# The second layer's MLP as seven block products: sums of blocks made ahead, middle blocks kept in DRAM

## The chip, the cores and the metric

One NeuronCore of a Trainium2 chip runs the whole two-layer network in one launch. The metric is the device time of that launch in microseconds (us), the median of several runs. Engines are named as in the profile: PE is TensorE's matmul, PEld its weight load, DVE is VectorE, ACT ScalarE, POOL GpSimd, SP SyncE, which here only issues DMAs.

## What is computed

The reference is a two-layer network on 256 context and 1024 latent tokens of width 1024. The part that the change rewrites is the MLP of the second layer (`layer == 1`), which runs on the 1024 latent tokens alone, and the norm before it and the last norm after it:

```python
hl2 = _modulate(_rmsnorm(xl, norm2_g[layer]), mod_l[3], mod_l[4])
xl = xl + mod_l[5] * _sqrelu_mlp(hl2, mlp_w1[layer], mlp_w2[layer])
...
return _rmsnorm(xl, final_g)

def _sqrelu_mlp(h, w1, w2):            # h 1024x1024, w1 1024x4096, w2 4096x1024, f32
    return jnp.square(jax.nn.relu(h @ w1)) @ w2
```

## The kernel before

Features lie on the 128 partitions and tokens on the free axis. A product in f32 precision is made of three fp32r matmuls: each operand is split in a high part, rounded to fp32r, and the rest, and high x high, high x low and low x high are added up in one PSUM bank. A weight tile of 128 x 1024 is loaded by SP into a `raw` buffer (`wprep`, L138), rounded by ACT into `w[:, 0]` (L140), and the rest goes by DVE into `w[:, 1]` (L141). We call these two a prep. `WStream` keeps two tiles prepared ahead of use (`fill`, `get`). `gemm` (L165) multiplies one weight tile with eight 128 x 512 token tiles: 24 matmuls (L170 to L172).

The MLP (`mlp`, L555) goes over 16 blocks `b` of 256 hidden features. For each it loads two tiles of w1 and two of w2. Up: per hidden tile and chunk of 512 tokens one `gemm`, then Relu, Square and a copy to high on ACT (L549 to L551) and the rest on DVE (L552). Down: `gemm2` (L508), per chunk and each of eight output tiles `d` six matmuls (L518 to L520), and `acc_x` (L501, L504) adds the bank times the gate to the residual `xl` on DVE. So the hidden never leaves the chip's SBUF. In the second layer there are two chunks (`LAT_CH`); the last two blocks run chunk by chunk, the second chunk in halves of 256 tokens (`tail`), so that the last norm (`final`, L1458) overlaps.

Norms are generators that are queued (`queue`, `K.bg`) and advanced a step or more at each `tick` between matmul groups: squares on ACT, sums on DVE (L187), four matmuls with ones (L192), a power on POOL (L195), transposes that spread it (L199), then DVE and ACT per tile. The norm of the second chunk before the MLP runs beside block 0 of the first chunk. In the first layer's MLP (`layer0_in`) the same `WStream.get` also takes a step of `K.side`: conditioning tiles (`ada_tile`, L82, L85) that DVE multiplies.

The order of instructions of an engine is made at build time by a scheduler that takes, of what it thinks is ready, the earliest written; priorities (`high_priority`) move some ahead. On the chip each engine's queue then runs in that order.

Of the kernel before, what the change touches and what calls it, by code (L numbers as in the profile page):

```python
# [19 lines left out]
NC_ = 256  # L20
NL = 1024
# [8 lines left out]


class Ctx:
    pass


def setup(ctx, tc, A):
    K = Ctx()
    nc = K.nc = tc.nc
    K.tc, K.A, K.side, K.bg, K.rate, K.nacc = tc, A, iter(()), iter(()), 0, 0
    PS = bass.MemoryType.PSUM  # L40
# [90 lines left out]


def wprep(K, src):
# [41 lines left out]

def rstd_steps(K, pool, xt, c0, n, ready=lambda: KT, evac=True):
    nc = K.nc
    while not ready():
        yield
    acc = pool.tile([128, 512], F32, name="nacc", tag="nacc", bufs=2)  # L180
    nc.scalar.activation(out=acc[:, :n], in_=xt[0][:, c0:c0 + n], func=AF.Square)
    for d in range(1, KT):
        while ready() <= d:
# [414 lines left out]
def tpool(K, name, bufs=1, side=None):  # L598
    return K.tc.tile_pool(name=name, bufs=bufs, side=side, reuse_waits="tile")
# [34 lines left out]
def queue(K, rate, *gens):  # L634
    K.rate, K.bg = rate, chain(K.bg, *gens)
# [17 lines left out]
def layer0_in(K, e0, dbg):  # L653
    nc, A = K.nc, K.A
    H, L = hl_tiles(K)
    apool = e0.enter_context(tpool(K, "ada"))
    with tpool(K, "n0") as np_:
        sT = np_.tile([128, KT, 2], F32, name="sT")
# [99 lines left out]
    with tpool(K, "t4") as p4:  # L758
# [551 lines left out]
def layer1(K, dbg, out):  # L1310
# [129 lines left out]
    if dbg in ("y1", "gla"):  # L1440
        xs.close()
        return
    with tpool(K, "n6") as np_:
        gemm2(K, 1, 2, [ws.get()], [(H[7], L[7])], xt, c0, n)
        queue(K, 3, norm_steps(K, np_, 1, 1, xt, c0, n))
        c0, n = LAT_CH[1]
        for d in range(KT):
            acc_x(K, 1, 2, d, xt, gemm(K, ws.get(), H, L, c0, n), c0, n)
        drain(K)
        queue(K, 0, norm_steps(K, np_, 1, 1, xt, c0, n))  # L1450
        with tpool(K, "t6") as p4, tpool(K, "wx6") as K.wx:
            tail = (LAT_CH[:1], ((NC_ + 512, 256), (NC_ + 768, 256)))
            mlp(K, p4, 1, xt, LAT_CH, 1, tail, 2, lambda c0, n, ready: final(K, np_, xt, out, c0, n, ready))
    xs.close()


def final(K, pool, xt, out, c0, n, ready):
    nc = K.nc  # L1458
    rs = yield from rstd_steps(K, pool, xt, c0, n, ready, False)
    for d in range(KT):  # L1460
# [138 lines left out]
```

## Time and profile before

| | us |
|---|---|
| median of 3 runs | 3169.49 (3165.36 to 3172.66) |
| span of the profiled execution | 3158.7 |
| PE busy | 3042.5 (96%) |
| DVE busy | 1954.3 (62%) |
| ACT busy | 1178.8 (37%) |
| POOL busy | 261.8 (8%) |
| DMA, mean | 91 GB/s |

The span is one execution, from the first to the last instruction; the median is of timed runs, which hold what lies around the span too. A busy time is the sum over an engine's instructions. PE's instructions are pipelined: one of 512 columns lasts 0.39 us and the next starts 0.23 us after it, so counts over time say more than busy shares.

### The profile page before, as it was taken

To read this page: it belongs to the slowest core of one execution; us is meant where nothing else is said; L and a number is where in the kernel's file an instruction comes from. 1 tells how busy PE (TensorE), PEld (TensorE's weight loads), DVE (VectorE), ACT (ScalarE), POOL (GpSimd) and SP (SyncE) were. 2 spreads that over 40 slices of the span, in tenths; PEclk is the share of its full clock that TensorE was granted. 3 is DMA by queue.
4 is the path that set the end of the run, shared out by engine and by line. 5 is a ranking of instruction groups with operands and counts; after the bars stand their busy time and mean duration, and the time that the engine had idled before them with its cause. 6 is when DMAs were issued, how large, how long until landed. Compare 5 with 4: busy or idle time off the path is not lost. (4 is left out here: it accounts for less than half of the span.)

```text
span 3158.7 us, 40982 instructions
## 1 busy us (share of the span) xinstructions
PE 3042.5 (96%) x15822; PEld 2519.1 (80%) x15822; DVE 1954.3 (62%) x3583; ACT 1178.8 (37%) x2132; POOL 261.8 (8%) x384
## 2 busy tenths in 40 slices
PE   8999999999999999999988999999999999999998
PEld 4778778888888888887766777888877788888887
DVE  5896666766545455458675658786877544444446
ACT  4774233422231222235553553443444322222224
POOL 1001110000000000001065440000020000000000
PEclk9999999999999999999999999999999999999999
DMA  6333134222222222113233332332372111111113
GB/s 233 116 123 113 44 111 138 73 81 80 73 81 67 90 71 80 41 64 131 89 100 98 109 103 71 104 107 91 114 240 94 60 47 54 47 47 40 54 62 106
DMA packets 159442, 288.16 MB, mean 91 GB/s; under 512 B 35360, under 2 KB 90080, under 8 KB 159120
## 3 DMA queue, kind: packets, MB, share of 16 engines
q1 hardware_dynamic: 151248, 258.01, 25.5%
q0 software_dynamic: 7856, 27.53, 2.7%
q8 instruction: 125, 2.05, 0.3%
q14 instruction: 69, 0.57, 0.1%
q10 hardware_dynamic: 144, 0.01, 0.0%
HBM read 239.35 MB, written 41.42 MB: 89 GB/s over the span
## 5 line engine op out<-in xcount | busy, mean ns | idle before, releaser
L171 PE MATMUL mm<-hL,w 128*128 128x512 f32 (+1 forms) x2840 | 1052.9, 371 | 1.1 <-DVE hL L223 0.8
L172 PE MATMUL mm<-hH,w 128*128 128x512 f32 (+1 forms) x2840 | 1050.3, 370 | 2.6 <-DVE w L141 2.6
L170 PE MATMUL mm<-hH,w 128*128 128x512 f32 (+1 forms) x2840 | 1049.9, 370 | 2.3 <-ACT px L498 1.4
L171 PEld LDWEIGHTS mm<-hL,w 128*128 128x128 f32 x2840 | 539.5, 190 | 86.1 <-issue 3.2
L170 PEld LDWEIGHTS mm<-hH,w 128*128 128x128 f32 x2840 | 538.8, 190 | 85.7 <-ACT px L498 2.2
L172 PEld LDWEIGHTS mm<-hH,w 128*128 128x128 f32 x2840 | 539.3, 190 | 83.9 <-DVE w L141 3.5
L140 ACT ACTIVATE w<-raw 128x1024 fp32r<-128x1024 f32 x241 | 250.3, 1053 | 702.3 <-PE mm L520 617.2
L518 PE MATMUL mm<-gH,w 128*128 128x512 f32 (+1 forms) x1312 | 475.0, 365 | 5.0 <-ACT gH L551 4.9
L520 PE MATMUL mm<-gH,w 128*128 128x512 f32 (+1 forms) x1312 | 479.6, 366 | 0.0
L519 PE MATMUL mm<-gL,w 128*128 128x512 f32 (+1 forms) x1312 | 478.4, 365 | 0.1
L141 DVE TENSOR_TENSOR w<-raw,w 128x1024 fp32r<-128x1024 f32 x241 | 292.2, 1224 | 165.5 <-ACT w L140 164.8
L504 DVE SCALAR_TENSOR_TENSOR px<-mm,mod,px 128x512 f32<-128x512 f32 (+1 forms) x408 | 264.5, 660 | 203.0 <-PE mm L520 190.3
L504 DVE SCALAR_TENSOR_TENSOR xl<-mm,mod,xl 128x512 f32<-128x512 f32 (+1 forms) x296 | 211.2, 720 | 180.6 <-PE mm L520 168.8
L518 PEld LDWEIGHTS mm<-gH,w 128*128 128x128 f32 x1312 | 245.9, 188 | 48.7 <-ACT gH L551 7.2
L519 PEld LDWEIGHTS mm<-gL,w 128*128 128x128 f32 x1312 | 246.4, 188 | 43.2 <-DVE gL L552 1.0
L520 PEld LDWEIGHTS mm<-gH,w 128*128 128x128 f32 x1312 | 246.5, 188 | 40.7
L549 ACT ACTIVATE gr<-mm 128x256 f32<-128x256 f32 (+1 forms) x164 | 89.5, 546 | 468.1 <-PE mm L172 462.3
L552 DVE TENSOR_TENSOR gL<-gr,gH 128x256 fp32r<-128x256 f32 (+1 forms) x164 | 102.3, 624 | 197.2 <-ACT gH L551 197.1
L85 DVE SCALAR_TENSOR_TENSOR sdummy<-raw,sbc 128x1024 bf16<-128x1024 f32 x128 | 156.5, 1223 | 93.3 <-DMA raw<-adaT 92.1
L951 POOL TENSOR_TENSOR gtp<-gsy 80x30 f32<-80x30 f32 (+14 forms) x120 | 80.5, 671 | 232.0 <-DMA rec<-gst 113.7
L195 POOL TENSOR_TENSOR nv<-nv,mhalf 128x4 f32<-128x4 f32 (+1 forms) x14 | 15.7, 1119 | 989.5 <-DVE nv L194 989.5
L551 ACT ACTIVATE gH<-gr 128x256 fp32r<-128x256 f32 (+1 forms) x164 | 95.2, 580 | 5.0
(340 smaller groups left out, 3178.9 us busy)
## 6 DMA issues: line engine op xcount, KB each, us to landing
raw<-w SPq DMA_DIRECT2D x152, 512.0 KB
raw<-adaT SPq DMA_DIRECT2D x80, 512.0 KB
raw<-odw SPq DMA_DIRECT2D x36, 512.0 KB
raw<-wout SPq DMA_DIRECT2D x33, 512.0 KB
grec<-rec SPq DMA_DIRECT2D x32, 384.0 KB
raw<-evw SPq DMA_DIRECT2D x20, 512.0 KB
adr<-adaw SPq DMA_DIRECT2D x16, 512.0 KB
rec<-gst SPq DMA_DIRECT2D x32, 256.0 KB
```

Of the source, the lines that this page charges most:

```text
L85: nc.vector.scalar_tensor_tensor(out=dummy, in0=r, scalar=1.0, in1=s[:, w, :], op0=MUL, op1=MUL, accum_out=K.mod[l][:, ft, w:w + 1])
L140: nc.scalar.activation(out=w[:, 0], in_=raw, func=AF.Copy)
L141: nc.vector.tensor_tensor(w[:, 1], raw, w[:, 0].bitcast(F32), SUB)
L170: nc.tensor.matmul(out, w[:, 0, k, :], h, start=(k == 0), stop=False)
L171: nc.tensor.matmul(out, w[:, 0, k, :], lo, start=False, stop=False)
L172: nc.tensor.matmul(out, w[:, 1, k, :], h, start=False, stop=(k == kn - 1))
L504: K.nc.vector.scalar_tensor_tensor(out=xt[d][:, c0:c0 + n], in0=ps, scalar=K.mod[l][:, 8 * m + d, wi:wi + 1], in1=xt[d][:, c0:c0 + n], op0 ...
L518: nc.tensor.matmul(o, w[:, 0, d, :], gH, start=(f == 0), stop=False)
L519: nc.tensor.matmul(o, w[:, 0, d, :], gL, start=False, stop=False)
L520: nc.tensor.matmul(o, w[:, 1, d, :], gH, start=False, stop=(f == last))
L551: nc.scalar.activation(out=gH[:, c0:c0 + n], in_=r[:, :n], func=AF.Copy)
L552: nc.vector.tensor_tensor(gL[:, c0:c0 + n], r[:, :n], gH[:, c0:c0 + n].bitcast(F32), SUB)
```

## The change

The two matrix products of the second layer's MLP are each cut in 2 x 2 blocks and made of seven block products (Strassen's, in Winograd's form) in place of eight.

Up: hidden tiles `2q` and `2q+1` are the two columns of blocks, tokens are cut in the two chunks and features in two halves. For each of 16 `q`, each block product is `up_prod`: 12 matmuls (four feature tiles). The sums of token blocks (`ops` 4, 6, 7) are made once, by `st_norm`. The sums of weight blocks are made per `q` in the stream (`quad_srcs`): four DVE operations of 512 columns. Products 1 and 2 of the first `PRE` = 8 `q` run first (`first_quad`), while the second chunk's norm (`st_norm`) is made, and their results go to DRAM; then `up_quad` makes the rest for q < 8 (five products), and all seven for the others. The hidden's blocks and their four sums (`t1` to `t4`) are made in f32 and stored to DRAM (`K.hop`) by POOL.

Down: seven products one after the other (`order`), each over 16 steps `q` of 12 matmuls. For each step one raw tile is loaded in two DMAs, half a block of w2 (or of its sums), half the hidden block, and split as one tile by one prep. Three weight tiles are prepared ahead, with five `w` and four `raw` buffers. Banks alternate between two sets of four; a bank's partial sums are added to up to three blocks of the residual, which is read back from DRAM (`xdr`).

The sums of w2's blocks (`wsum_steps`) are made during the first layer's MLP: 32 steps, each two loads and a store by POOL and four DVE operations of 256 columns, one step at a `get`.

```diff
+    K.sdr = [[K.dram.tile([128, 4, 512], F32, ...) for q in range(NQ)] for w in range(2)]
+    K.hop = {p: [K.dram.tile([128, 512], F32, ...) for q in range(NQ)] for p in range(1, 8)}
...
 def wprep(K, src):
-    raw = K.wr.tile([128, KT, 128], F32, name="raw", tag="raw")
-    nc.sync.dma_start(out=raw, in_=src)
+        for lo, hi, ap in parts:
+            nc.sync.dma_start(out=raw[:, lo:hi], in_=ap)
+def quad_srcs(K, l, q, first):
...
+    def sums():
+        a = st[0] if first else load(0)
+        b = load(1)
+        s = rawt(K)
+        tt(s[:, 4:8], a[:, 0:4], b[:, 0:4], SUB)
+        tt(b[:, 0:4], b[:, 0:4], b[:, 4:8], ADD)
+        tt(s[:, 0:4], b[:, 0:4], a[:, 0:4], SUB)
+        tt(a[:, 4:8], a[:, 4:8], s[:, 0:4], SUB)
+        return s
+    return ([lambda: load(0)] if first else []) + [sums, lambda: st[1], lambda: st[0][:, 4:8]]
...
 class WStream: def get(self):
+                if self.K.last is not None:
+                    with self.K.tc.issue_after(self.K.last):
+                        next(self.K.side2, None)
...
 layer1:
+        with tpool(K, "n6") as np_, tpool(K, "pre") as pp:
...
+            ws = WStream(K, [A["w1"][1, 2 * q] for q in range(PRE)])
+            queue(K, 2, st_norm(K, np_, 1, xt, 1, ops))
+            for q in range(PRE):
+                first_quad(K, pp, ws.get(), q, ops)
+            drain(K)
+        K.wx = xs.enter_context(tpool(K, "wx7", side="right"))
+        rx = xs.enter_context(tpool(K, "rx7", 2, side="right"))
+        ws = WStream(K, [s for q in range(NQ) for s in quad_srcs(K, 1, q, q >= PRE)], K.wx, raws=(rx, rx))
+            for q in range(NQ):
+                up_quad(K, hp, ws, q, ops)
+        down(K, 1, xt, wx8, rx, lambda ...: final(...))
-            tail = (LAT_CH[:1], ((NC_ + 512, 256), (NC_ + 768, 256)))
-            mlp(K, p4, 1, xt, LAT_CH, 1, tail, 2, lambda ...: final(...))
+def st_norm(K, pool, l, xt, ci, ops):
+    for d in range(KT):
+        nc.gpsimd.dma_start(out=K.xdr[:, d, ...], in_=xt[d][:, c0:c0 + n])
+    rs = yield from rstd_steps(K, pool, xt, c0, n, nb=1)
...
+    for j in range(4):                 # ci == 1
+        scale(j)
+        nc.vector.tensor_tensor(x11, x12, x11, SUB)
+        scale(j + 4)
+        split(K, x22, ops[3][j], sB(j + 4))
+        stt(x12, x22, df[:, j:j + 1], x12)
+        stt(x22, x22, sB(j + 4), x11)
+        split(K, x22, ops[6][j])
+        stt(x21, x21, sB(j + 4), x22)
+        split(K, x12, ops[7][j])
+        split(K, x11, ops[5][j])
+        split(K, x21, ops[4][j])
+def up_quad(K, pool, ws, q, ops):      # here q < PRE
+        nc.sync.dma_start(out=p1, in_=K.p1dr[q])
+        nc.sync.dma_start(out=h11, in_=K.hop[1][q])
+        w = ws.get(); b2 = mm_tile(K)
+        up_prod(K, b2, w, 0, ops[6], True, False)
+        tt(u2, b2, p1, ADD)
+        w3 = ws.get(); b3 = mm_tile(K)
+        up_prod(K, b3, w3, 0, ops[5], True, False)
+        up_prod(K, b2, w, 1, ops[7], False, False)
+        tt(u3, b2, p1, ADD)
+        tt(h22, b3, u3, ADD)
+        up_prod(K, b4, ws.get(), 0, ops[3], True, True)
+        tt(u2, b3, u2, ADD)
+        tt(h12, b4, u2, ADD)
+        up_prod(K, b2, w3, 1, ops[4], False, True)
+        tt(h21, b2, p1, ADD)
...
+    for h in (h22, h21, h12):
+        sq_relu(K, h, h)
+    tt(t1, h12, h11, SUB); tt(t3, h22, h12, SUB); tt(t2, h22, t1, SUB); tt(t4, h21, t2, SUB)
+    for p, t in ((2, h21), (3, h22), (5, t1), (7, t3), (6, t2), (4, t4)):
+        nc.gpsimd.dma_start(out=K.hop[p][q], in_=t)
+def down(K, l, xt, wx, rx, after):
+    order = (1, 6, 2, 7, 5, 4, 3)
+    src = [[(0, 4, wop(p, q)), (4, 8, K.hop[p][q]...)] for p in order for q in range(NQ)]
+    ws = WStream(K, src, K.wx, wx, wx, ahead=3, raws=(rx, rx))
+    for c0, n in LAT_CH:
+        for d in range(KT):
+            nc.sync.dma_start(out=xt[d][:, c0:c0 + n], in_=K.xdr[:, d, ...])
+    for p in order:
...
+        for q in range(NQ):
+            w = ws.get()
+            rh, rl = (w[:, i, 4:8].rearrange("p k c -> p (k c)") for i in range(2))
+            for d in range(4):         # three matmuls each, into bank[key][d]
...
+        if p == 1:
+            for d0, c0 in ((0, a1), (4, a1), (4, a0)):
+                acc("A", d0, c0)
...
+        else:                          # p == 3, the last
+            drain(K)
+            K.nacc = 4
+            queue(K, 3, urgent(K, after(a1, n, lambda: K.nacc, (4, 5, 6, 7, 0, 1, 2, 3))))
+            acc("A", 0, a1)
+            drain(K)
```

The last norm of the second chunk now runs in one piece of 512 tokens, four of its eight tiles ahead of the last product's end.

## Rows read from the trace of the kernel before

**Rows 1.** The page's first part: busy time, share of the span and count of instructions of each engine.

```profile
PE 3042.5 (96%) x15822; PEld 2519.1 (80%) x15822; DVE 1954.3 (62%) x3583; ACT 1178.8 (37%) x2132; POOL 261.8 (8%) x384
```

**Rows 2.** The view by windows: window, its length, then busy us and (count) of PE, PEld, DVE, ACT, POOL, the granted PE clock, the DMA engines' busy share and GB/s. The second layer's MLP as a whole, 600 us of its middle, and 40 us near its start.

```profile
2426.00:3145.00 719.00, 712.80 (x3293) 588.06 (x3291) 345.51 (x462) 207.90 (x312) 2.94 (x2) 1.00 0.18 57
2500.00:3100.00 600.00, 599.89 (x2622) 489.60 (x2621) 270.44 (x340) 157.06 (x226) 0.00 (x0) 1.00 0.16 51
2440.00:2480.00 40.00, 34.95 (x150) 27.21 (x151) 30.68 (x42) 15.16 (x21) 1.28 (x1) 1.00 0.20 66
```

**Rows 3.** The view of waits, of PE from 2380 us to the end: engine, tile, line, whom it waited for, us in all, times, longest.

```profile
PE sm L199 <- POOL nv L195: 5.3, 4, 2.2
PE mm L518 <- ACT gH L551: 2.7, 1, 2.7
PE mm L171 <- DVE hL L223: 0.8, 1, 0.8
```

**Rows 4.** The timeline: start us, duration, engine, line, operation, out<-in, shape, then the idle time before and what ended it. Two matmuls that follow each other just before the MLP, ACT's first Relu of the MLP, and two matmuls late in it.

```profile
2424.05 0.39 PE L171 MATMUL mm<-hL,w 128*128 128x512 f32 x1
2424.27 0.39 PE L172 MATMUL mm<-hH,w 128*128 128x512 f32 x1
...
2431.50 0.60 ACT L549 ACTIVATE gr<-mm 128x512 f32<-128x512 f32 x1 [2.86 <-PE mm L172]
...
3083.86 0.40 PE L170 MATMUL mm<-hH,w 128*128 128x512 f32 x1
3084.09 0.39 PE L171 MATMUL mm<-hL,w 128*128 128x512 f32 x1
```

**Rows 5.** The view of groups by line and shape, from 2432 us to the end: count, busy us, mean ns of one, then the engine's idle time before them and what ended it.

```profile
L141 DVE TENSOR_TENSOR w<-raw,w 128x1024 fp32r<-128x1024 f32 x73 | 87.7, 1220 | 81.5 <-ACT w L140 81.5
L140 ACT ACTIVATE w<-raw 128x1024 fp32r<-128x1024 f32 x73 | 75.1, 1052 | 276.9 <-PE mm L520 276.8
L550 ACT ACTIVATE gr<-gr 128x512 f32<-128x512 f32 x60 | 37.6, 626 | 0.8
```

**Rows 6.** The timeline of DVE in three places where it runs without a gap: from one start to the next is what an instruction takes up of the engine.

```profile
2408.75 0.74 DVE L220 SCALAR_TENSOR_TENSOR nt<-xl,modA,nrs 128x512 f32<-128x512 f32 x1
2409.42 0.69 DVE L187 TENSOR_TENSOR nacc<-nacc,nsq 128x512 f32<-128x512 f32 x1
2410.02 0.74 DVE L504 SCALAR_TENSOR_TENSOR xl<-mm,mod,xl 128x512 f32<-128x512 f32 x1
...
3122.17 1.22 DVE L141 TENSOR_TENSOR w<-raw,w 128x1024 fp32r<-128x1024 f32 x1
3123.30 2.06 DVE L1462 SCALAR_TENSOR_TENSOR xl<-xl,gn,sm 128x512 f32<-128x512 f32 x3
...
3142.28 0.41 DVE L187 TENSOR_TENSOR nacc<-nacc,nsq 128x256 f32<-128x256 f32 x1
3142.61 0.48 DVE L504 SCALAR_TENSOR_TENSOR xl<-mm,mod,xl 128x256 f32<-128x256 f32 x1
```

**Rows 7.** The view by windows again, in the mixer before the MLP, where PE waits for a chain on DVE and ACT (columns as in Rows 2).

```profile
2254.00:2256.00 2.00, 1.04 (x6) 0.66 (x6) 1.69 (x6) 0.37 (x1) 0.00 (x0) 1.00 0.41 142
2256.00:2258.00 2.00, 0.68 (x5) 0.49 (x4) 1.86 (x12) 0.00 (x0) 0.00 (x0) 0.64 0.11 26
2258.00:2260.00 2.00, 1.48 (x5) 1.15 (x6) 1.82 (x3) 0.37 (x1) 0.00 (x0) 0.50 0.42 171
2260.00:2262.00 2.00, 2.00 (x8) 1.65 (x7) 1.36 (x2) 0.00 (x0) 0.00 (x0) 0.50 0.61 193
2262.00:2264.00 2.00, 2.00 (x8) 1.65 (x8) 1.56 (x5) 0.33 (x2) 0.00 (x0) 0.65 0.34 113
2264.00:2266.00 2.00, 2.00 (x11) 1.62 (x10) 2.00 (x4) 1.29 (x7) 0.21 (x1) 1.00 0.45 162
```

**Rows 8.** The view by windows in the stretch of the span in which DMA is busiest.

```profile
2305.00:2335.00 30.00, 26.04 (x147) 20.12 (x145) 20.64 (x47) 13.51 (x29) 9.07 (x17) 1.00 1.01 358
```

**Rows 9.** The view of the residual's tile `xl`: its 16 loads of 256 KB that POOL issues one upon the other in the stretch of Rows 8 (ns of POOL that an issue takes, shortest, median, longest), and the time from issue to landing.

```profile
L1428 POOL DMA_DIRECT2D xl<-xdr x16: 537/537/542, 2310.8 to 2323.4; - x16
...
DMA to landing us min/median/max: 5.4/7.6/9.0
```

**Rows 10.** The view of `raw` in the MLP: SP's issues of w1 and w2 (ns of one, shortest, median, longest).

```profile
L138 SPq DMA_DIRECT2D raw<-w x55: 327/328/328, 2503.2 to 3077.5; - x55
```

**Rows 11.** The timeline of the end, all engines but PEld: the last matmul of the MLP, its last sum, the spreading of the last norm's factor, and the last products with it.

```profile
3144.39 0.28 PE L520 MATMUL mm<-gH,w 128*128 128x256 f32 x1
...
3144.79 0.48 DVE L504 SCALAR_TENSOR_TENSOR xl<-mm,mod,xl 128x256 f32<-128x256 f32 x1
...
3148.76 0.69 PE L199 MATMUL sm<-cm,nv 128*128 128x128 f32 x2 [1.10 <-POOL nv L195]
3149.49 5.18 DVE L1462 SCALAR_TENSOR_TENSOR xl<-xl,gn,sm 128x256 f32<-128x256 f32 x13 [0.78 <-PE sm L199]
```

**Rows 12.** The view by windows in the first layer's MLP (columns as in Rows 2).

```profile
640.00:1100.00 460.00, 460.00 (x2409) 395.84 (x2408) 252.48 (x381) 117.29 (x191) 0.00 (x0) 1.00 0.24 78
```

**Rows 13.** The view of the tensor `adaT`: who waits for the loads of the side work, for how many us in all, and how often.

```profile
  DVE sdummy L85: 92.1, 58
```

More of the change, by code (lines that the diff above doesn't have):

```diff
@@ L61, in setup @@
     K.xdr = K.dram.tile([128, KT, NL], F32, name="xdr")
+    K.sdr = [[K.dram.tile([128, 4, 512], F32, name=f"sdr{w}{q}") for q in range(NQ)] for w in range(2)]
+    K.hop = {p: [K.dram.tile([128, 512], F32, name=f"hop{p}{q}") for q in range(NQ)] for p in range(1, 8)}
+    K.p1dr = [K.dram.tile([128, 512], F32, name=f"p1dr{q}") for q in range(PRE)]
     return K
@@ L130, in ada_cols, with rawt @@
             in1=K.gn[:, 0, f0 - 8:f0 - 4].unsqueeze(2).to_broadcast([128, 4, 2]), op0=ADD, op1=MUL)
+def rawt(K):
+    t = K.rl[K.ri % len(K.rl)].tile([128, KT, 128], F32, name="raw", tag="raw")
+    K.ri += 1
+    return t
 def wprep(K, src):
@@ L173, in gemm, with rstd_steps @@
     return out
-def rstd_steps(K, pool, xt, c0, n, ready=lambda: KT, evac=True):
+def rstd_steps(K, pool, xt, c0, n, ready=lambda: KT, evac=True, order=tuple(range(KT)), nb=2):
     nc = K.nc
@@ L179, in rstd_steps @@
         yield
[L180 to L183, printed above, removed]
+    acc = pool.tile([128, 512], F32, name="nacc", tag="nacc", bufs=nb)
+    nc.scalar.activation(out=acc[:, :n], in_=xt[order[0]][:, c0:c0 + n], func=AF.Square)
+    for i in range(1, KT):
+        d = order[i]
+        while ready() <= i:
             yield
@@ L201, in rstd_steps @@
         return pb
-    rs = pool.tile([128, 512], F32, name="nrs", tag="nrs", bufs=2)
+    rs = pool.tile([128, 512], F32, name="nrs", tag="nrs", bufs=nb)
     nc.scalar.activation(out=rs[:, :n], in_=pb[:, :n], func=AF.Copy)
@@ L768, in layer0_in @@
         mlp(K, p4, 0, xt, OUT_CH, 2, (OUT_CH[:2], OUT_CH[2:]), 1, after)
+        for _ in chain(K.side, K.side2):
+            pass
     return xt
@@ new lines, in layer1, with wsum_steps, load @@
+    with tpool(K, "xm") as xp_, tpool(K, "wx8", 2) as wx8, tpool(K, "n8") as np_:
+        xt = [Shifted(xp_.tile([128, NL], F32, name=f"xm{d}"), NC_) for d in range(KT)]
+        down(K, 1, xt, wx8, rx, lambda c0, n, ready, order: final(K, np_, xt, out, c0, n, ready, order))
+    xs.close()
+def wsum_steps(K, l):
+    nc = K.nc
+    todo = [(1, q, hf) for q in range(NQ) for hf in range(2)]
+    def load(i, q, hf):
+        raw = K.sr.tile([128, KT, 128], F32, name="sraw", tag="sraw")
+        for f in range(2):
+            src = K.A[("w1", "w2")[i]][l, 2 * q + f].rearrange("p (s k) c -> p s k c", s=2)[:, :, 2 * hf:2 * hf + 2]
+            nc.gpsimd.dma_start(out=raw[:, 4 * f:4 * f + 4].rearrange("p (s k) c -> p s k c", s=2), in_=src)
+        return raw
+    raw = load(*todo[0])
+    yield
+    for n, (i, q, hf) in enumerate(todo):
+        b = [raw[:, 2 * j:2 * j + 2] for j in range(4)]
+        a11, a12, a21, a22 = b if i == 0 else (b[0], b[2], b[1], b[3])
+        tt = nc.vector.tensor_tensor
+        tt(a22, a21, a22, ADD)
+        tt(a21, a11, a21, SUB)
+        tt(a11, a22, a11, SUB)
+        tt(a12, a12, a11, SUB)
+        nc.gpsimd.dma_start(out=K.sdr[i][q][:, :, 256 * hf:256 * hf + 256],
+                            in_=raw.rearrange("p (j k) c -> p j (k c)", j=4))
+        if n + 1 < len(todo):
+            raw = load(*todo[n + 1])
+        yield
@@ new lines, in up_prod, with mm_tile @@
+def up_prod(K, ps, w, half, op, first, last):
+    nc = K.nc
+    for k in range(4):
+        h, lo = op[k]
+        i = 4 * half + k
+        nc.tensor.matmul(ps, w[:, 0, i, :], h, start=(first and k == 0), stop=False, skip_group_check=True)
+        nc.tensor.matmul(ps, w[:, 0, i, :], lo, start=False, stop=False, skip_group_check=True)
+        nc.tensor.matmul(ps, w[:, 1, i, :], h, start=False, stop=(last and k == 3), skip_group_check=True)
+    tick(K)
+def mm_tile(K):
+    return K.pmm.tile([128, 512], F32, name="mm", tag="mm")
@@ new lines, in sq_relu, with first_pair @@
+def sq_relu(K, dst, src):
+    nc = K.nc
+    nc.scalar.activation(out=dst, in_=src, func=AF.Relu)
+    nc.scalar.activation(out=dst, in_=dst, func=AF.Square)
+def first_pair(K, pool, w, q, ops, between=lambda p1: None):
+    nc = K.nc
+    b1 = mm_tile(K)
+    up_prod(K, b1, w, 0, ops[1], True, False)
+    p1 = pool.tile([128, 512], F32, name="sp1", tag="sp1", bufs=2)
+    nc.scalar.activation(out=p1, in_=b1, func=AF.Copy)
+    between(p1)
+    up_prod(K, b1, w, 1, ops[2], False, True)
+    h11 = pool.tile([128, 512], F32, name="sh11", tag="sh11", bufs=2)
+    sq_relu(K, h11, b1)
+    nc.gpsimd.dma_start(out=K.hop[1][q], in_=h11)
+    return p1, h11
@@ L1461, in final @@
+def final(K, pool, xt, out, c0, n, ready, order=tuple(range(KT))):
+    nc = K.nc
+    rs = yield from rstd_steps(K, pool, xt, c0, n, ready, False, order)
+    for d in order:
         t = xt[d][:, c0:c0 + n]
```

170 lines of the change are left out of this document (150 added, 20 removed).

## The prediction

> **What bounds the kernel now.** Read the page's busy shares first [rows 1]: PE at 96% is the engine to look at, DVE at 62% the next. Then the windows of the second layer's MLP [rows 2]: PE is busy 712.8 of 719 us at full clock, DVE under half, DMA at 57 GB/s. In the middle 2622 matmuls start in 600 us, one every 0.229 us (the timeline shows steps of 0.22 and 0.23 [rows 4]). The MLP has 3072 matmuls of 512 columns, or as many columns in halves at the end: 2 products x 32 hidden tiles x 8 x 2 chunks x 3. At 0.229 us that is 703.5 us. The first hidden tile's 24 matmuls end where ACT's first Relu starts, at 2431.5, so they began at 2426.0 [rows 4]; the last ends at 3144.7 [rows 11]. So of 718.7 us some 15 are lost, most near the start, where 40 us hold 150 matmuls in place of 175 [rows 2]; the waits name few of them [rows 3]. PE alone sets this stretch, so fewer matmuls are time, if the rest can be fed.
>
> **What is removed.** Seven products in place of eight leave 7/8 of the matmuls: 2 x 16 x 7 x 12 = 2688. At 0.229 us: 615.6 us. This is 103 us under today's stretch, of which 88 are matmuls and 15 today's losses. Everything below is what the new stretch loses. For the step I allow 1%, 6 us, either way.
>
> **What an instruction of DVE costs.** From start to start a TENSOR_TENSOR of 512 columns takes 0.60 us, a SCALAR_TENSOR_TENSOR 0.67, the prep's 1024 columns 1.13, and 256 columns 0.33 [rows 6]. Reads of PSUM in TENSOR_TENSOR do not occur in these rows; I take 0.67, as for L504, which reads a bank. ACT takes 1.05 us for a prep and 0.63 for 512 columns [rows 5].
>
> **From the first 8 q to the rest.** While products 1 and 2 of eight `q` run (192 matmuls, 44 us), the second chunk's norm must be made, with its sums of blocks. The factor `rs` comes out after five `tick`s, since the matmuls with ones are written behind the fourth product: 5 x 2.75 us and an ACT copy, 14.4 us. Then DVE has per `j` six operations of 0.67 and five of 0.60, 7.0 us, four times: 28. Between them stand four preps, 4.5. That ends at 47, 3 us behind PE. Then the four sums of the first `quad_srcs`, 2.4, and ACT's prep, 1.05, with hops 51: PE stands for 7 us, since its next product needs that tile. In the mixer a gap of about 2.5 us within 4 us is followed by windows granted 0.64, 0.50, 0.50 and 0.65, so at the lower level of 1.2 GHz for a part of 8 us [rows 7]; the time lost by that is (0.36 + 0.50 + 0.50 + 0.35) x 2 = 3.4 us. I take 7 + 3.4 = 10.5; bounds 4 (some sums slip in earlier) and 18 (ACT, 0.9 loaded there by my count, holds up the splits).
>
> **The up product, q < 8.** Per quad PE has 60 matmuls, 13.7 us. DVE has the four sums and `t1` to `t4`, 8 x 0.60, six evacuations, 6 x 0.67, preps of 1.13, 1.13 and 0.6: 11.7 us, 85%. Within the quad each accumulation on a bank waits for a DVE read of it, and one product (2.75 us) lies between as cover. The prep of `b` for the next quad needs the buffer that product 4, the quad's last, frees: 1.05 + 1.22 us of ACT and DVE against 2.75 until product 5. If an evacuation comes behind that prep on DVE, the cover is overrun: 1.05 + 1.22 + 3 x 0.67 = 4.3 against 2.75, 1.5 us. The scheduler avoids some of it. The nearest rows with DVE this loaded are the 40 us near the MLP's start: DVE 77%, 25 matmuls missing, 5.7 us or 14% [rows 2], though part of it is a norm's chain. 14% of 110 us is 15. Bounds 0 and 20; I take 1 us a quad, 8. For q >= 8 PE has 84 matmuls, 19.2 us, DVE 12.2 (one prep more, one evacuation less), 63%, and two products of cover in most places: 3 us for eight quads, bounds 0 and 10. POOL's six or seven issues a quad at 0.54 us [rows 9] are under 4 us of 13.7; bytes are 3 MB in 13.7 us, 219 GB/s, under the 358 that the span shows [rows 8].
>
> **From up to down.** The first down tiles need `w` buffers freed by products 4 and 3 of the last quad, one of them a product ahead: covered but for small change. SP also loads the residual, 16 x 256 KB, 4.2 MB, some of it only when product 4 has freed the space. At 358 GB/s [rows 8] all of it takes 11.7 us, and stands in the queue ahead of the next weight tiles, but three tiles (8 us) are prepared and half of the residual's space is free early. I take 2, bounds 0 and 12.
>
> **The down product.** 112 steps of 2.75 us. ACT 1.05, DVE 1.13 and 36 sums of 0.67 spread over 308 us: half loaded. SP issues two DMAs at 0.33 [rows 10]. Bytes: 0.52 MB a step, 191 GB/s, against 57 today [rows 2] and 358 at most. Four `raw` buffers turn round in landing plus prep: with the 7.6 us at which 256 KB landed under full load [rows 9], (7.6 + 1.05 + 1.22 + 0.3) / 4 = 2.5 us, under the step; with the longest, 9.0, it is 2.9 and costs 112 x 0.15 = 17. At 191 GB/s they should land sooner. I take 2, bounds 0 and 17. The seven changes of banks are covered by a product of 44 us on the other set.
>
> **The end.** From the last matmul's end to the span's end are 14.0 us today [rows 11]. With 512 columns the last sum, square and add take 0.75 us more, two more columns of L192 and L199 0.6, eight products of 0.66 as long as today's 13 of 256 columns, the last store 0.3 more: +1.8.
>
> **The first layer.** 32 steps of 4 x 0.33 us, 43 us of DVE, in a stretch of some 455 us where DVE is idle for 45% and PE never [rows 12]. DMA goes from 78 to about 150 GB/s. Per block two `get`s follow each other at once, so a step's operations can stand on DVE waiting for a load issued just before; behind them are the sums of L504, for which PE's banks wait. DVE already waits 58 times, 92 us in all, for such loads [rows 13], and PE shows no loss. So little: I take 4; bounds 0 and 40 (eight times 5 us, the shortest landing of rows 9). Issues on POOL block no power there: no norm runs in these steps.
>
> **The sum.** 615.6 + 10.5 + 8 + 3 + 2 + 2 = 641 for 718.7: -77.6. With +1.8 and +4: -71.8. The profiled span of 3158.7 becomes 3087; the median lies 10.8 above the span, so 3169.5 - 71.8 = 3098.
>
> **Rivals.**
> (a) Almost nothing is exposed: DVE and DMA keep up, only half of the gap after the first 8 q stays. Then 5 + 19 us less is lost, 3074. For it: DVE is below 100% in every stretch but one. Against: 3 us of PE's cover per wait.
> (b) The up product is set by DVE's order. Each of 16 quads loses 2 us and after it the clock, 3.4 us more [rows 7]: 16 x 5.4 = 86 in place of 11, 3173, no change; where both waits of a quad fall behind a prep it is slower. It would decide from 5.2 us a quad. Against it: for q >= 8 DVE has a third of its time free, and PE's gaps would be shorter than in rows 7.
> (c) The first layer's sums hold up PE at each pair of `get`s and the down product's loads land at 9 us: 36 + 15 more, 3149. Half of it is likelier than all: 3125.
> (d) Slower: the down product is set by its loads. If the two DMAs of a tile land one behind the other, each at the 7.6 us of rows 9, the turn of four buffers is (15.2 + 2.6) / 4 = 4.4 us a step, 1.7 over PE, 112 x 1.7 = 190 in place of 2: 3286. It decides from a landing of 11.1 us for both: (11.1 + 2.6) / 4 is 0.66 over the step, and 112 x 0.66 eats the gain and the 2 us above. Against it: in rows 8 many transfers of this size are in flight at once and 358 GB/s come out. The Trainium skill (DMA: Bandwidth & Descriptors, "Anatomy of one DMA" and "Bandwidth") speaks for it: a DMA costs some 2.0 us besides its bytes and loads should be of 1 MiB or more, and this change halves today's 512 KB. By its formula, an estimate, 256 KB take 2.6 us, two in a row 5.2 against a step of 2.75, and the down product alone would lose 275 us; rows 8 contradict that loads wait for each other.
>
> **Chances.** The forecast and what is near it, 3080 to 3115: 0.58. (a): 0.13. (c) and the space up to 3163: 0.18. (b): 0.06, half no change, half slower. (d): 0.05. A measurement of this kernel tells about 0.2%, 6.3 us, from no change. So faster 0.89, same 0.03, slower 0.08. The range leaves out (d), (b), the end of (c) and what lies under (a), 0.19 together: 3068 to 3145.
>
> **What would show it.** Right: 2688 matmuls of 512 columns in the MLP; PE gaps of 7 to 10 us once, after the 16th product, with a window at a lower granted clock behind it, ended by DVE's sums and ACT's prep; gaps near 1 us per quad, ended by DVE; the down product at 2.75 us a step with ACT's prep waiting for PE, not for DMA; the first layer's windows as full as today. Wrong: if in the down product ACT's prep waits for loads step after step, (d); if quads are 16 us and more, (b); if PE in 640 to 1100 us shows gaps, (c); if matmuls start further apart than 0.229 us without a wait, for 190 to 220 GB/s into the same memory, a price of which I have no row beyond 358 GB/s in a stretch where PE stood still anyway.

## The result, and the profile after

The changed kernel takes 3089.27 us (median of 4 runs, 3085.7 to 3092.11), the kernel before, run beside it, 3167.43 (4 runs, 3165.36 to 3172.66): a ratio of 0.9747, with a 95% interval of 0.9733 to 0.9761. Forecast was 3098, so the change brings 78 us where 72 were expected. The profiled span goes from 3158.7 to 3083.9 us, by 74.8; each is one execution, and the one profiled before the change was a short one (see the sum, below).

The page's first part, as [rows 1]; PE still sets the time:

```profile
PE 2959.9 (96%) x15246; PEld 2444.0 (79%) x15246; DVE 2062.2 (67%) x3736; ACT 1256.8 (41%) x2176; POOL 403.5 (13%) x615
```

The windows (columns as in [rows 2]): the first layer's MLP, which answers to [rows 12]; the last 38 us of the norm beside the first products; what follows it; the up quads of q < 8; all up quads; the seam between up and down; the rest of the down product.

```profile
640.00:1100.00 460.00, 460.00 (x2401) 395.40 (x2400) 295.62 (x509) 114.09 (x185) 65.97 (x92) 1.00 0.45 149
2448.00:2486.00 38.00, 32.74 (x132) 23.85 (x132) 36.68 (x53) 27.11 (x45) 6.59 (x13) 0.99 0.53 173
2480.00:2490.00 10.00, 6.35 (x21) 4.32 (x20) 7.47 (x10) 4.38 (x6) 0.54 (x1) 0.83 0.48 159
2500.00:2600.00 100.00, 100.00 (x440) 82.33 (x439) 87.60 (x125) 49.64 (x69) 23.66 (x44) 1.00 0.65 223
2487.00:2761.00 274.00, 274.00 (x1196) 224.77 (x1195) 198.73 (x271) 126.67 (x177) 56.09 (x104) 1.00 0.55 191
2760.00:2770.00 10.00, 3.67 (x12) 2.24 (x11) 1.86 (x2) 2.78 (x3) 0.00 (x0) 0.76 0.84 325
2772.00:3067.00 295.00, 295.00 (x1301) 242.91 (x1299) 162.76 (x159) 118.26 (x118) 1.04 (x1) 1.00 0.59 191
```

In the two long stretches a matmul starts every 0.229 us, as before [rows 2], though DMA moves 191 GB/s there instead of 51 to 57: 274 / 1196 in the first, and 295 / 1289 in the second, where 12 of the 1301 are short ones of the last norm (L237, L244). Ahead of the last matmul PE loses time in two places alone, around the end of the first products (2448 to 2490) and at the seam (2760 to 2770). The waits of PE from 2400 us on name them (columns as in [rows 3]):

```profile
PE mm L1747 <- ACT w L159: 6.3, 1, 6.3
PE sm L237 <- DVE nacc L232: 3.6, 1, 3.6
PE mm L1618 <- ACT w L159: 3.4, 1, 3.4
```

L1618 is the first matmul of an up product, L1747 of a down product, L159 the prep on ACT. The 3.4 us stand is the one behind the first 8 `q`. The 6.3 us stand is at the seam, and the timeline shows who is late there:

```profile
2746.00 11.41 SPq L1727 DMA_DIRECT2D xm<-xdr  x16
2758.43 0.33 SPq L156 DMA_DIRECT2D raw<-w  x1
...
2766.90 1.06 ACT L159 ACTIVATE w<-raw 128x1024 fp32r<-128x1024 f32 x1 [13.13 <-DMA raw<-hop]
2768.01 1.22 PE L1747 MATMUL mm<-w 128*128 128x512 f32 x2 [6.29 <-ACT w L159]
...
3066.64 0.39 PE L1749 MATMUL mm<-w 128*128 128x512 f32 x1
...
3070.65 1.87 PE L237 MATMUL sm<-cm,nacc 128*128 128x1 f32 x8 [3.61 <-DVE nacc L232]
3073.86 1.12 PE L244 MATMUL sm<-cm,nv 128*128 128x128 f32 x4 [1.34 <-POOL nv L240]
```

SP issues the residual's 16 loads (L1727) one after the other, 11.4 us; behind them stands the next weight tile's load (L156), whose prep starts 8.5 us after it was issued, so four steps into the down product PE has nothing prepared. ACT, the engine that PE is said to wait for, was idle for 13.1 us itself; what is late is the load, first in SP's queue and then behind the residual's 4.2 MB. The last three rows are the end of the kernel, to be held against [rows 11].

Stage by stage, profile against profile (before, after):

| stretch | before | after | difference |
|---|---|---|---|
| start of the kernel to the first load of `evw`, a weight of the first stage | 35.7 | 39.3 | +3.6 |
| from there to the first down matmul of the first layer's MLP | 561.4 | 561.3 | -0.1 |
| to its last | 874.8 | 874.6 | -0.2 |
| to the second layer's first up matmul | 954.1 | 956.9 | +2.8 |
| the second layer's MLP | 718.7 | 634.9 | -83.8 |
| its last matmul's end to the span's end | 14.0 | 16.9 | +2.9 |

### The profile page after: what moved, and what is told of

Its sections match the earlier page's. It is cut to its first block, busy times and chain, and to the rows that moved or that the text cites. A ratio compares the mean times of both kernels' runs of the same rounds, so it can differ in the third digit from the quotient of the medians.

```text
span 3083.9 us, 41065 instructions
## 1 busy us (share of the span) xinstructions
PE 2959.9 (96%) x15246; PEld 2444.0 (79%) x15246; DVE 2062.2 (67%) x3736; ACT 1256.8 (41%) x2176; POOL 403.5 (13%) x615
## 5 line engine op out<-in xcount | busy, mean ns | idle before, releaser
L216 PE MATMUL mm<-hH,w 128*128 128x512 f32 (+1 forms) x2296 | 845.2, 368 | 3.3 <-DVE w L160 3.3
L215 PE MATMUL mm<-hL,w 128*128 128x512 f32 (+1 forms) x2296 | 847.6, 369 | 0.0
L214 PE MATMUL mm<-hH,w 128*128 128x512 f32 (+1 forms) x2296 | 844.8, 369 | 2.1 <-ACT px L543 1.4
L159 ACT ACTIVATE w<-raw 128x1024 fp32r<-128x1024 f32 (+1 forms) x341 | 351.6, 1037 | 714.2 <-PE mm L565 340.4
L160 DVE TENSOR_TENSOR w<-raw,w 128x1024 fp32r<-128x1024 f32 (+1 forms) x341 | 407.4, 1202 | 245.0 <-ACT w L159 243.0
L216 PEld LDWEIGHTS mm<-hH,w 128*128 128x128 f32 x2296 | 437.6, 191 | 65.2 <-DVE w L160 4.2
L214 PEld LDWEIGHTS mm<-hH,w 128*128 128x128 f32 x2296 | 436.8, 190 | 64.8 <-ACT px L543 2.2
L565 PE MATMUL mm<-gH,w 128*128 128x512 f32 (+1 forms) x768 | 273.2, 356 | 0.0
L564 PE MATMUL mm<-gL,w 128*128 128x512 f32 (+1 forms) x768 | 272.4, 355 | 0.1
L563 PE MATMUL mm<-gH,w 128*128 128x512 f32 (+1 forms) x768 | 269.2, 353 | 2.3 <-ACT gH L596 2.3
L563 PEld LDWEIGHTS mm<-gH,w 128*128 128x128 f32 x768 | 144.0, 188 | 24.7 <-ACT gH L596 3.1
L564 PEld LDWEIGHTS mm<-gL,w 128*128 128x128 f32 x768 | 144.0, 188 | 22.7 <-DVE gL L597 0.6
L565 PEld LDWEIGHTS mm<-gH,w 128*128 128x128 f32 x768 | 144.4, 188 | 19.3
L1747 PE MATMUL mm<-w 128*128 128x512 f32 x256 | 100.6, 394 | 6.3 <-ACT w L159 6.3
L1618 PE MATMUL mm<-hH,w 128*128 128x512 f32 x256 | 100.6, 394 | 0.9 <-ACT sp L1639 0.7
L1620 PE MATMUL mm<-hH,w 128*128 128x512 f32 x256 | 100.2, 393 | 1.1 <-DVE w L160 1.1
```

Of the source, the lines that this page charges most:

```text
L159: nc.scalar.activation(out=w[:, 0, :n], in_=raw, func=AF.Copy)
L160: nc.vector.tensor_tensor(w[:, 1, :n], raw, w[:, 0, :n].bitcast(F32), SUB)
L214: nc.tensor.matmul(out, w[:, 0, k, :], h, start=(k == 0), stop=False)
L215: nc.tensor.matmul(out, w[:, 0, k, :], lo, start=False, stop=False)
L216: nc.tensor.matmul(out, w[:, 1, k, :], h, start=False, stop=(k == kn - 1))
L563: nc.tensor.matmul(o, w[:, 0, d, :], gH, start=(f == 0), stop=False)
```

## The experiments

All start from the changed kernel. "Up" is from the first up matmul to the first down matmul, "down" from there to the start of the last: 318.5 and 316.0 us in the changed kernel, 634.5 together. Each run but the last is a single one. They are compared by these two stretches, since single whole times also carry what differs from run to run ahead of the MLP: with the residual spread out, with twelve first `q` and with late sums the whole takes 3088.29, 3085.92 and 3090.19 us, and shows none of the three gains by itself. In runs whose edit leaves it alone up takes 318.5 to 319.8 us and down 312.2 to 316.5, as the stand at the seam lasts 3.1 to 6.7 us.

**The residual's loads spread out.** Is the seam SP's queue, or the space that the loads need?

```diff
-    for c0, n in LAT_CH: for d in range(KT): nc.sync.dma_start(out=xt[d][...], in_=K.xdr[...])
...
+            if p == 1 and 1 <= q <= 8:         # behind the newest weight load
+                for d, c0 in todo[2 * q - 2:2 * q]: nc.sync.dma_start(...)
```

> The 16 loads of the residual are issued two at a time behind the weight loads of steps 1 to 8 of the first down product, in place of all ahead of the down product's fourth weight tile. Theory: PE's stand between the up and the down product (6.3 us, and some 8.4 us with the slow clock behind it) comes from SP's queue, where the 16 issues and their 4.2 MB stand ahead of the next weight tiles. Then the stand goes, under 1 us is left, and from the up product's end to the last matmul 7 to 9 us less pass. Rival 1: the stand is the turnover of ACT and DVE at the end of the last quad: it stays above 5 us. Rival 2: the loads collide wherever they stand, since the first down product needs 191 GB/s already: the stand is shared out over the first eight steps, which take 2.9 us or more each in place of 2.72.

Down takes 307.4 us, 8.6 less; up 319.5. The stand is gone, though the same bytes are moved beside the down product's first steps:

```profile
2762.30:2784.00 21.70, 21.70 (x96) 17.75 (x96) 12.72 (x13) 9.04 (x11) 2.70 (x5) 1.00 0.98 350
```

PE is full while DMA moves 350 GB/s. So not the bytes but their place ahead of the weight tiles made the seam. Spreading takes away both the late issue and the landing behind the residual, 8.5 us; which of them costs more was not tried apart. And 1344 matmuls at 0.229 are 307.8: behind the seam the down product loses nothing.

**Twelve first `q`, and four.** The first products cover the second chunk's norm. The number of `q` that they are made of, `PRE`, was set to 12, then to 4.

> Products 1 and 2 of 12 q run first, in place of 8, so PE has 66 us in place of 44 to cover the second chunk's norm. Theory: DVE's count of the norm sets the end of that stretch (about 49 us behind the MLP's start, and 2.4 + 1.05 us more). Then PE's stand of 3.4 us and the slow clock behind it go; from the MLP's start to the last matmul 4 to 8 us less. Rival: each quad of five products costs PE gaps, and four more of them (12 in place of 8, DVE 85% loaded) give the gain back: the time stays within 2 us or rises, with gaps ended by DVE in the quads 8 to 11.

> The first stretch of up products (the q before the modulated norm is ready) is cut from 8 to 4, so TensorE has some 22 us of work there and not 44. Theory: the norm of the second layer's MLP is counted out by VectorE and ends some 49 us after the first up product whatever the length of this stretch, so TensorE's stand behind it grows from 3.4 us to about 26, and from the first up product to the last down product it takes 15 to 20 us more than 634.5. Rival: the stand comes from the weight stream starting again behind the stretch; then it stays at 3 to 4 us and the total within 2 us of 634.5.

With 12 the stand of 3.4 us goes, but up takes 316.7, only 1.8 less and still 8.9 over its matmuls: what PE loses during the norm stays, and the first quads behind it now lose time (20 us from 2507.3 hold 77 matmuls, 10 fewer than at 0.229). Up and down together fall by 5.2 to 629.3, in the range expected, but by luck: 3.4 of that is the seam, which was shorter in this run and which the edit does not touch. With 4 the waits and windows are:

```profile
PE mm L1618 <- ACT w L159: 23.4, 1, 23.4
```

```profile
2460.00:2470.00 10.00, 0.60 (x3) 0.18 (x1) 9.81 (x16) 5.81 (x10) 0.54 (x1) 0.70 0.36 113
2470.00:2480.00 10.00, 0.00 (x0) 0.00 (x0) 9.93 (x16) 4.68 (x8) 0.00 (x0) 0.50 0.18 70
2480.00:2490.00 10.00, 5.92 (x17) 4.32 (x18) 7.08 (x10) 2.64 (x4) 0.00 (x0) 0.60 0.32 101
```

PE stands for 23.4 us while DVE is full, and its next product starts 48.2 us after the first; with 8 it was 53.0. So it is DVE's count of operations that ends this stretch, and the restart of the weight stream is refuted as its cause. Up and down together take 648.2, 13.7 more, under the 15 to 20 expected: the norm ends 4.8 us earlier, which the four preps fewer between its operations on DVE (4 x 1.13) would make, and the seam's stand was 3.2 here.

**The first layer's sums held back.** In the changed kernel the scheduler put the first loads of `wsum_steps` at the start of the kernel. The timeline of POOL in the changed kernel:

```profile
1.28 3.06 POOL L1527 DMA_DIRECT2D sraw<-w  x4 [0.84 <-POOLq L1838]
```

```diff
-                    with self.K.tc.issue_after(self.K.last):
+                    with self.K.tc.issue_after(self.K.last), self.K.tc.issue_after(self.K.lastx):
...
-            nc.gpsimd.dma_start(out=xt[d][:, :T], in_=A["xT"][:, d, :])
+            K.lastx = nc.gpsimd.dma_start(out=xt[d][:, :T], in_=A["xT"][:, d, :]).ins
```

> All loads for the sums of w2 are held back on POOL's queue until the first layer's residual has been loaded; nothing else changes. Theory: the 3.6 us by which the first weight tile of the first layer is loaded later than before (39.3 in place of 35.7 us) come from the first 1 MB of these loads, which now run at 1.3 us, where DMA is full: they go, and the first load of evw starts at 36 us again. Rival: the start just varies from run to run: it lies anywhere between 35 and 40 us, though no sraw load is near. In both, the first layer's MLP takes as long as before (some 887 us from the first to the last use of its hidden).

The tile's rows now begin at 476.1 us in place of 1.3:

```profile
L1527 POOL DMA_DIRECT2D sraw<-w x64: 704/716/737, 476.1 to 1080.9; - x64
```

SP's first load of `evw` is issued at 36.6 us. In the nine runs with the early loads it is at 37.8 to 41.1, before the change at 35.7, and in the last experiment below, which holds them back too, at 36.3. So the four early loads, 1 MB, cost some 3 us at the start. That it reaches the end can't be read from this run: its stretch from there to the first layer's MLP took 568.3 us in place of 561.3. This stretch differs from run to run, 561.3 to 569.3 in the nine with the early loads and 554.9 in the last experiment. The first layer's MLP itself takes 876.1 with the late loads and 874.6 with the early ones, 874.8 before: no price of the sums there.

**Two `raw` buffers in the down product.** How far is rival (d)?

```diff
-    ws = WStream(K, src, K.wx, wx, wx, ahead=3, raws=(rx, rx))
+    ws = WStream(K, src, K.wx, wx, wx, ahead=3)
```

> The down product's stream has two raw buffers in place of four. Theory (each buffer turns round in landing plus prep, 2.6 us): a step takes (L + 2.6) / 2 where that is above PE's 2.72. With a landing of the pair of 256 KB loads of 3.5 us that is 3.05 us a step, 37 us more in all; from L = 2.9 us it begins to cost. Rival (loads wait in queues, L of 7.6 us as 256 KB took in the busiest stretch of the kernel before): 5.1 us a step, 265 us more. If there is no cost, L is under 2.9 us and four buffers were never needed.

Down takes 370.9, 54.9 more; 37 were expected. The waits of ACT from 2800 to 3100 us show the expected cause, and the timeline of SP and ACT a pair of loads from its issue at 2902.08 to its prep at 2906.08 (the prep between is of the other buffer):

```profile
ACT w L159 <- DMA raw<-hop: 184.6, 87, 7.8
```

```profile
2902.08 0.33 SPq L156 DMA_DIRECT2D raw<-w  x1
2902.46 0.42 SPq L156 DMA_DIRECT2D raw<-hop  x1
2902.95 1.06 ACT L159 ACTIVATE w<-raw 128x1024 fp32r<-128x1024 f32 x1 [2.16 <-DMA raw<-hop]
...
2906.08 1.06 ACT L159 ACTIVATE w<-raw 128x1024 fp32r<-128x1024 f32 x1 [2.07 <-DMA raw<-hop]
```

A step takes (370.9 - 8.6) / 112 = 3.23 us on average; two buffers turn round in 6.47, of which 2.6 are preps and hops, so a tile's two DMAs land in 3.9 us together, not in 15.2 as rival (d) has it. The expectation had taken 3.5 for it. If they land as soon with four buffers, these turn in (3.9 + 2.6) / 4 = 1.6 us a step, under the 2.75 of PE; there the preps wait for PE and not for loads, so this landing can't be read from them.

**Every load of the down product twice.** The second load goes to buffers that nothing reads.

```diff
             w = ws.get()
+            dm = K.rd.tile([128, KT, 128], F32, ...)
+            for lo, hi, ap in src[...]: nc.sync.dma_start(out=dm[:, lo:hi], in_=ap)
```

> In each step of the down product the two loads are made a second time into a spare ring of four buffers that nothing reads: 1.05 MB a step in place of 0.52. Theory: loads overlap, so the step is bound by bytes: at the 358 GB/s of the busiest stretch before 2.93 us, 0.2 us over PE's 2.72, 20 to 25 us in all, with the DMA share at 1.0; at 390 GB/s, the most seen in 5 us, nothing. Rival (loads wait for each other): a pair of loads that takes 5 us or more, and a step of 5 us: 250 us more.

Down takes 336.2, 20.2 more, as expected. Here the DMA engines are full:

```profile
2900.00:3000.00 100.00, 96.67 (x423) 79.03 (x423) 48.12 (x46) 38.39 (x39) 0.00 (x0) 1.00 1.00 360
2960.00:2980.00 20.00, 20.00 (x89) 16.51 (x88) 8.39 (x7) 6.75 (x7) 0.00 (x0) 1.00 1.00 354
```

At 360 GB/s the 1.05 MB of a step take 2.91 us, 0.16 over PE's step, 18 in 112. But the loss does not come step by step, as the second row shows. Behind the seam it comes where products end. The waits of PE from 2800 to 3070 us come first here, then DVE's twelve sums of the first product, which stand ahead of the longest wait's prep:

```profile
PE sm L1751 <- DVE w L160: 10.3, 3, 7.0
PE mm L1751 <- DVE w L160: 3.9, 3, 1.7
```

```profile
2810.06 7.99 DVE L549 SCALAR_TENSOR_TENSOR xm<-mm,mod,xm 128x512 f32<-128x512 f32 x12 [3.31 <-PE mm L1752]
```

The changed kernel has the same 8.0 us of sums, from 2801.2 on, and no wait of PE from 2800 to 3066 us, so there the tiles prepared ahead cover them; with DMA full they no longer did. The changed kernel's 191 GB/s are about half of what this stretch bears.

**Four more sums per quad on DVE.** The sums `t1` to `t4` are made twice.

```diff
     tt(t4, h21, t2, SUB)
+    tt(t1, h12, h11, SUB); tt(t3, h22, h12, SUB); tt(t2, h22, t1, SUB); tt(t4, h21, t2, SUB)
```

> DVE makes the hidden's four sums t1 to t4 twice in each quad of the up product, the same values: 2.4 us more per quad. Theory: the up product is PE's as long as DVE's sum per quad stays under PE's, since the order of its queue leaves cover for each wait. For q < 8 DVE then has 14.1 us against PE's 13.7, so these quads grow to DVE's: 0.4 us each, 3 us in all, with DVE at 100%; for q >= 8 (14.6 against 19.2) nothing. Rival (each accumulation waits behind whatever stands on DVE): four more operations at each quad's end push the evacuations of the next quad back, 1.5 us or more in each of 16 quads, 24 us or more.

Up takes 321.7, 3.2 more where 3 were expected, for 64 operations that take 38 us of DVE. DVE is nearly full, and PE begins to lose:

```profile
2500.00:2600.00 100.00, 99.46 (x432) 80.15 (x431) 95.56 (x144) 42.62 (x63) 21.37 (x40) 1.00 0.61 205
```

So the quads of q < 8, at 87.6% of DVE, still had 12.4% of 13.7, 1.7 us of DVE each, to spare, and the order on DVE does not hold PE: rival (b) is refuted for this kernel.

**Two buffers for the up weights in place of three.** What kept the quads free of gaps?

```diff
-        ws = WStream(K, [...quad_srcs...], K.wx, raws=(rx, rx))
+        ws = WStream(K, [...quad_srcs...], raws=(rx, rx))
```

> The up products' prepared weights get two buffers instead of three; nothing else changes. Theory: a weight's preparation (rounding and a sum, about 2.0 us on ScalarE or VectorE) lies behind a product only because the third buffer is free before it; with two, the quads of q below 8, where most weights are prepared sums, show two uncovered preparations of some 2 us each, 32 us more from the first up product to the first down product (318.5), and the quads from 8 on nothing. Rival 1: the order of the instructions hides them all the same; under 8 us more. Rival 2: the quads from 8 on lose as much; up to 64 us more.

Up takes 344.7, 26.2 more; 32 were expected. The waits of PE from 2430 to 2780 us:

```profile
PE mm L1618 <- ACT w L159: 10.2, 13, 3.4
PE mm L1618 <- DVE raw L180: 7.3, 3, 2.5
```

The loss is where it was expected: the 100 us from 2500 hold 347 matmuls, those from 2640 are full (437). The waits name 17.5 us, 3.4 of them the stand that the changed kernel has too, so 14.1 of the 26.2. Slow matmuls make up at least a part of the rest, in windows and then in the timeline of PE:

```profile
2510.00:2520.00 10.00, 9.28 (x41) 7.38 (x40) 4.84 (x8) 1.96 (x4) 2.16 (x4) 1.00 0.65 234
2520.00:2530.00 10.00, 7.32 (x25) 5.23 (x24) 8.60 (x12) 4.35 (x6) 2.70 (x5) 0.83 0.61 193
```

```profile
2523.84 0.50 PE L1618 MATMUL mm<-to,w 128*128 128x512 f32 x1 [2.46 <-DVE raw L180]
...
2527.01 0.63 PE L1618 MATMUL mm<-to,w 128*128 128x512 f32 x1
2527.44 0.63 PE L1619 MATMUL mm<-to,w 128*128 128x512 f32 x1
```

Behind a gap of 2.5 us matmuls start 0.43 us apart for some 3 us, in a window granted 0.83, so a short wait here costs more than its length.

**The last down product twice.** One product's price in place, with all its loads and preps and no sums between the two:

```diff
-    order = (1, 6, 2, 7, 5, 4, 3)
+    order = (1, 6, 2, 7, 5, 4, 3, 3)     # banks start at the first, are read after the second
```

The output's last block thus holds that product twice.

> The last product of the down product is run a second time into the same banks, with its loads and preps, as an eighth product, so the block of the output that it goes to holds it twice. Theory: a product is worth PE's time for 192 matmuls: 16 x 2.72 = 43.6 us more, so the two products that the change takes away are worth 87 us and the losses at the seams take the rest. Rival (the steps are fed by DMA and preps, and PE just fits): an added product costs clearly more than 44 us, or the steps show waits on ACT.

Down takes 359.9, 43.9 more; 192 matmuls at 0.229 are 44.0. So this product costs its matmuls and nothing beside.

**The three repairs together.** Late residual, twelve first `q`, late sums.

> The late residual loads, the 12 first q and the late sums of w2 together. Theory: the three losses stand at different places and add up: 8.5 at the seam to the down product, 2 to 5 at the end of the first products, 3.3 at the start: 14 to 17 us under the changed kernel, some 3073 us, ratio to the kernel before 0.970. Rival: the start varies by itself, so only 10 to 12 us are left: 0.9715.

3075.15 us (median of 5, 3063.43 to 3080.53) against 3169.73 for the kernel before (8 runs): 0.9707, 0.9690 to 0.9725, outside the changed kernel's interval and 14 us less. Up and down together take 624.4, 10.1 less, and `evw` starts 3.0 us earlier: 13.1 of the 14. Down alone is 307.4 again. The profiled execution is the fastest of the five, though, 22.2 us shorter in its span than the changed kernel's: 6.4 of that lie between `evw` and the first layer's MLP and 2.3 between the two MLPs, where no edit is.

## Why the prediction was right, and by which steps

**Matmuls.** 615.6 forecast; at the measured pitches 1344 x 0.2291 + 1344 x 0.2289 = 615.5. The fear of a longer pitch at 190 to 220 GB/s fell: the changed kernel, and the run at 350 GB/s with PE full, show none. This term carries the gain, and the doubled product shows that it is worth what it was costed at.

**After the first 8 `q`.** 10.5 forecast. In the first 49.6 us 44.0 would have done: 5.6 lost while DVE is full (the window from 2448), of which the waits name 1.8; then the stand of 3.4; then slow matmuls, 23 missing in the 10 us from 2481.7, 5.3 with the stand. Together 10.9, and up is 10.7 over its matmuls. The size was right, and the cause of the stand (a chain on DVE that outlasts PE's work) is shown by the run with four. But in the forecast's own terms the chain ended 53.0 us after the first product's start and not 51, and the clock cost 1.9 and not 3.4; the two errors cancel. And it lay elsewhere in part: nothing was forecast inside the norm, where half of it was.

**Up quads.** 8 + 3 forecast, 0 measured (440 matmuls in 100 us, at 87.6% of DVE). This step was mis-sized: it was taken from the 40 us near the MLP's start [rows 2], whose loss, as in the changed kernel's own 38 us, came with a norm's chain. What keeps the quads free of it is the third weight buffer, which the stream of the kernel before has too (`wx6`, L1451): with two buffers the quads of q < 8 lose 26.2 / 8 = 3.3 us each, where rival (b) had 5.4.

**From up to down.** 2 forecast, 8.6 measured, inside the bound of 12: 6.3 of it the stand, the rest slow matmuls behind it (granted clock 0.76). The bound was the right mechanism, loads that stand ahead of the next weight tile, and the value taken was mis-sized: I let three prepared tiles cover them. PE ran through four steps while SP still issued and the loads landed.

**The down product.** 2 forecast, -0.4 measured behind the seam (307.4 for 307.8). As forecast the prep waits for PE there, not for loads. The waits of ACT from 2775 to 3066 us in the changed kernel:

```profile
ACT w L159 <- PE mm L1749: 82.6, 51, 2.6
ACT w L159 <- PE sm L1749: 69.5, 42, 1.7
ACT w L159 <- DMA raw<-hop: 8.3, 6, 5.6
```

The 7.6 us of [rows 9], from which its bound and rival (d) came, are of sixteen loads queued at once; the pair here lands in 3.9, and in 8.5 behind the residual's sixteen. The rule of the Trainium skill that the prediction set against the change (DMA: Bandwidth & Descriptors, "Bandwidth", loads of 1 MiB or more) did not decide: loads of 256 KB came at 191 GB/s without a wait of PE, and at 350 to 360 when asked for. The formula that the prediction took from the Trainium skill (DMA: Bandwidth & Descriptors, "Anatomy of one DMA") stands there for DMAs that POOL issues, while SP issues these; by measure a pair lands in 3.9 us and not in 5.2.

**The end.** +1.8 forecast, +2.9 measured. From the last matmul's end to the spreading of the factor it is 6.8 us now (L244), 4.1 before [rows 11]: 2.7 of the 2.9. I had counted three terms there, 0.75, 0.6 and 0.66; which one is larger was not measured apart.

**The first layer.** +4 forecast, in the MLP. There it cost nothing, as [rows 12] had let hope: 460.00 of 460 us at 149 GB/s. It cost some 3 us at a place that I had not looked at, the kernel's start, since the scheduler takes what is ready and the first loads of the sums were ready at once. I had looked at POOL's queue in the steps of the MLP only, and did not follow it back to the first instruction.

**The sum.** Forecast 641 for the MLP, measured 634.9; -74.8 between the spans for -71.8. The terms' errors are -11 for the up quads, +6.6 for the seam and -2.4 for the down product. They cancel in part, so that the total came out this close is partly luck. The 2.8 us between the two MLPs stay open: that stretch took 954.4 to 959.4 us in the ten runs above, 954.6 with all three repairs, so it is not tied to an edit. Nor was the 10.8 us between median and span a constant, as I used it: it is 5.4 after the change. What lies around a span is less: each run on record is 1.7 to 2.0 us longer than its own span. The rest is that the profiled executions were short ones, by some 9 us before the change and 3.6 after it, so the medians, with -78, are the better measure of the change. Executions of kernels that start alike differ by up to 8 us ahead of the first layer's MLP (561.3 to 569.3, above).

**Rivals.** (a) was near for the quads and the down product, but not for the seam and the norm. (b) and (d) were refuted by experiment, (c) by the profile.

## What to carry to other kernels

Count matmuls first, then list every place where a stream of prepared tiles starts, ends or is refilled: in this kernel the long stretches lost nothing, and the loss was in two seams. Look in a queue for the block of loads that isn't needed yet but stands ahead of the one that is, and spread it out; 8.6 us came back here from a few lines. When new work has no input of its own to wait for, look where the scheduler puts its first instruction.

## What the runs showed of the hardware that was not expected

Operations of one form differ in pace. Among DVE's sums of weight blocks (L177 to L180) one starts 0.72 us after the other, while the hidden's (L1704, L1705) take up 0.60, both 128 x 512 in f32 with all operands in SBUF and with the same 0.69 us of duration. The timeline of DVE in the changed kernel:

```profile
2561.21 0.69 DVE L178 TENSOR_TENSOR raw<-raw 128x512 f32<-128x512 f32 x1
2561.94 0.69 DVE L179 TENSOR_TENSOR raw<-raw 128x512 f32<-128x512 f32 x1
2562.66 0.69 DVE L180 TENSOR_TENSOR raw<-raw 128x512 f32<-128x512 f32 x1
...
2571.77 0.69 DVE L1704 TENSOR_TENSOR st<-sh,sh 128x512 f32<-128x512 f32 x1
2572.37 0.69 DVE L1705 TENSOR_TENSOR st<-sh,st 128x512 f32<-128x512 f32 x1
2572.97 0.69 DVE L1666 TENSOR_TENSOR su<-mm,sp 128x512 f32<-128x512 f32 x1
```

L179 reads what L178 has just written, and L180 what L179 has; L1705 and L1666 don't read what the operation before them wrote. The same trace has the same operations in another order:

```profile
2645.05 0.69 DVE L177 TENSOR_TENSOR raw<-raw 128x512 f32<-128x512 f32 x1
2645.78 0.69 DVE L178 TENSOR_TENSOR raw<-raw 128x512 f32<-128x512 f32 x1
2646.39 0.69 DVE L1693 TENSOR_TENSOR su<-mm,sp 128x512 f32<-128x512 f32 x1
2646.99 0.68 DVE L179 TENSOR_TENSOR raw<-raw 128x512 f32<-128x512 f32 x1
...
2658.11 0.68 DVE L1705 TENSOR_TENSOR st<-sh,st 128x512 f32<-128x512 f32 x1
2658.83 0.69 DVE L1706 TENSOR_TENSOR st<-sh,st 128x512 f32<-128x512 f32 x1
```

With L1693 in between, the next operation starts 0.61 us behind L178 and L179 0.60 behind L1693, while L1706, which reads the result of L1705, starts 0.72 behind it. It is so each time in this trace: L178 to L179 0.71 to 0.73 (12 times), L178 to L1693 0.61 to 0.68 (4); L1705 to L1706 0.72 to 0.78 (9), L1705 to L1666 0.60 (7). So here the pace goes with what the next operation needs, not with the operation. L178 does not read what L177 wrote; it overwrites what L177 reads, and starts 0.72 to 0.73 behind it (13 times). Three such pairs make the weight sums 0.36 us a quad dearer than the 0.60 that they were costed at. And a clock that had fallen did not rise while PE stood: in the run with four first `q` the granted clock was 0.50, the 1.2 GHz level, through 10 us in which PE ran nothing, 0.60 in the next 10 with 17 matmuls, and 1.00 after them.
